# A planner's rule for VectorE and GpSimd, widened to VectorE's copies and tensor_scalars from SBUF

## The chip, the cores and the metric

The kernel runs on one core of a Trainium2 chip. The metric is the device time of one execution in microseconds (us); of several runs the median counts.

## What is computed

Two post-norm layers of a diffusion backbone over 512 latent tokens and 256 context tokens, 1024 wide, in 32-bit floats. Cut to what matters here:

```python
for l in range(2):
    hx, hc = modulate(xs, x_sh1, x_sc1), modulate(cs, c_sh1, c_sc1)   # shifts and scales from c, c_ctx @ w_ada
    aq, ak, av, bq, bk, bv, cq, ck, cv = split_proj(hx @ w_in[l])     # the same for hc
    aq, ak, bq, bk = rope_2d(...)                                     # latent tokens only
    ya = window_gqa(aq, ak, av, akc, avc, sink[l])                    # group A, 6 heads of 64
    yb = diff_attention_latent(bq, bk, bv, bkc, bvc, lam, ...)        # group B, 4 heads of 2 x 32
    yc = neighbourhood_attention(cq, ck, cv, ckc, cvc, na_bias[l])    # group C, 6 heads of 64
    xn = post_norm(xs, concat(ya, yb, yc) @ w_o[l], ...)
    xs = post_norm(xn, swiglu(modulate(xn, ...), w_ffn_in[l], w_ffn_out[l]), ...)
    if l == 0: cs = the same for the context tokens
```

## The kernel before

Activations lie transposed in SBUF, features on the partitions. The large tile R holds every operand of the projections as a pair of rounded numbers, a high part and a low part (what the rounding left), so that a product takes three TensorE passes: high x high, high x low, low x high (`gemm_step`, line 618). A weight block of 128x1024 comes by DMA into WRB or V; ScalarE rounds it into R and GpSimd subtracts to get the low part (`halves`, lines 583 to 588). This subtract is called a split below; it is on GpSimd alone.

Per layer the stages are: the projections of a group of heads (`proj`, line 798) and its attention (`attend`, line 1025), A, then B, then C, overlapped with each other; the output projection; LayerNorm; the feed-forward network. In `proj`, each head's result in PSUM, or after the rotation in the tile TRB, becomes a unit of R in three steps: ScalarE copies it with rounding (the high part; lines 858 and 869), that high part is copied once more within R (`va.tensor_copy`, lines 859 and 870: "va" means that VectorE or ScalarE may do it), and the low part is a subtract of two operands (lines 860 and 872: "vp" is VectorE or GpSimd, "ve" is VectorE alone). Units of group B have 32 rows, those of A and C 64; latent streams are 512 words wide and context streams 256. In `attend`, VectorE makes the negated maxima of the scores, TensorE transposes them, and a one-row cast (line 1044, again "va") puts them into R for the next matmuls.

No instruction is issued where it is written. Every call is recorded as an `Op` (`Program.add`, line 228) with the engines that may do it and a planned duration for each. `Program.schedule` (line 276) then plays a list schedule: whenever an engine is free, it takes the first operation of that engine's list that is ready. What it finds is the fixed order of each engine's queue. Where TensorE is planned to wait, `keep_busy` puts matmuls of constant data (`mean_w`, issued at line 1408) in, as fillers. So all instructions of the profile carry line 400 (the call in `issue`), the memsets line 398, the fillers line 1408; groups are told apart by their tiles.

For VectorE and GpSimd the planner holds a flag `two`: set where an operation has the operands `in0` and `in1`, both in SBUF. Such an operation is not started on VectorE while such a one is planned to run on GpSimd, nor the other way round if it could go elsewhere; a split, which can't, is started and planned longer by the overlap.

Of the kernel before, what the change touches and what calls it, by code (L numbers as in the profile page):

```python
# [187 lines left out]
class Program:  # L188
# [39 lines left out]
    def add(self, alt, args, kw):  # L228
        o = Op()
        idx = len(self.ops)  # L230
        o.kw = dict(kw)
        if args:
            o.kw["ap"] = args[0]
            o.kw["constant"] = args[1]
        o.key = idx
        o.succ, o.slots = [], []
        pre = set()
        seen = set()
        for k, v in o.kw.items():
            if not isinstance(v, (View, bass.AP)):  # L240
                continue
            if isinstance(v, View) and id(v.slot) not in seen:
                seen.add(id(v.slot))
                o.slots.append(v.slot)
                v.slot.left += 1
            w = k in ("out", "accum_out", "ap")
            for c in self.cells(v):
                if c in self.writer:
                    pre.add(self.writer[c])
                if w:  # L250
                    pre.update(self.readers.get(c, ()))
        for k, v in o.kw.items():
            if not isinstance(v, (View, bass.AP)):
                continue
            w = k in ("out", "accum_out", "ap")
            for c in self.cells(v):
                if w:
                    self.writer[c] = idx
                    self.readers[c] = []
                else:  # L260
                    self.readers.setdefault(c, []).append(idx)
        if self.after is not None:
            pre.add(self.after)
        pre.discard(idx)
        o.wait = len(pre)
        for p in pre:
            self.ops[p].succ.append(idx)
        o.alt = {e: (call, duration(e, call.__name__, o.kw), RANK[e].get(self.kind, 3)) for e, call in alt}
        o.eng = alt[0][0]
        o.ready = 0.0  # L270
        o.two = all(k in o.kw and self.sbuf(o.kw[k]) for k in ("in0", "in1"))
        o.kind = self.kind
        o.start = None
        self.ops.append(o)

    def schedule(self):
        ops = self.ops
        free = {e: 0.0 for e in ENG}
        avail = {e: [] for e in ENG}

        def offer(i):
            for e, (_, _, r) in ops[i].alt.items():
                insort(avail[e], (r, i))
        for i, o in enumerate(ops):
            if o.wait == 0:
                offer(i)
        dma, table = 0.0, 0
        twice = {"dve": 0.0, "pool": 0.0}
        ev = [0.0]
        left = len(ops)  # L290
        t = 0.0
        while left:
            if not ev:
                raise RuntimeError("the schedule is stuck")
            t = heapq.heappop(ev)
            while ev and ev[0] <= t:
                heapq.heappop(ev)
            for e in ENG:
                if free[e] > t:
                    continue  # L300
                got = None
                if len(avail[e]) > 40:
                    avail[e] = [q for q in avail[e] if ops[q[1]].start is None]
                for j, (_, i) in enumerate(avail[e]):
                    o = ops[i]
                    if o.ready > t or o.start is not None:
                        continue

                    if o.two and (e == "dve" and twice["pool"] > t or e == "pool" and twice["dve"] > t and len(o.alt) > 1):
                        continue  # L310
                    places = []
                    ok = True
                    for s in o.slots:
                        if s.place is None:
                            pl = s.ring.find(s, t)
                            if pl is None:
                                ok = False
                                break
                            places.append((s, pl))
                    if ok:  # L320
                        got = j
                        break
                if got is None:
                    continue
                avail[e].pop(got)
                for s, pl in places:
                    s.ring.take(s, pl, t)
                o.start, o.eng = t, e
                o.call, o.dur = o.alt[e][:2]
                if e == "pe" and t < COLD:  # L330
                    o.dur *= 2

                if o.two and e in ("dve", "pool"):
                    x = "pool" if e == "dve" else "dve"
                    o.dur += max(twice[x] - t, 0.0)
                    twice[e] = t + o.dur
                left -= 1
                if e == "sp":
                    free[e] = t + 0.5
                    dma = max(dma, t + 1.1) + o.dur  # L340
                    o.end = dma + 0.8
                else:
                    if e == "act":
                        f = TABLE.get(o.kw.get("func"), table)
                        if f != table:
                            table = f
                            o.dur += 1.28
                    free[e] = o.end = t + o.dur
                heapq.heappush(ev, free[e])
                for s in o.slots:  # L350
                    s.left -= 1
                    s.t = max(s.t, o.end + 0.2)
                    if s.left == 0:
                        s.ring.release(s, s.t)
                        heapq.heappush(ev, s.t)
                for q in o.succ:
                    n = ops[q]
                    n.wait -= 1
                    n.ready = max(n.ready, o.end + SYNC[e].get(n.eng, 0.0))
                    if n.wait == 0:  # L360
                        offer(q)
                        heapq.heappush(ev, n.ready)
        self.end = max(o.end for o in ops)
# [54 lines left out]
def duration(eng, name, kw):  # L418

    out = kw["out"] if "out" in kw else kw["ap"]  # L420
    n = words(out)
    inp = next((kw[k] for k in ("in0", "in_", "rhs") if k in kw), out)
    a = inp.ap if isinstance(inp, View) else inp
    psum = a.space == bass.MemoryType.PSUM
    ptrs = sum(isinstance(kw.get(k), (View, bass.AP)) for k in ("scalar", "scalar1", "scalar2", "bias", "scale"))
    if eng == "pe":
        w = kw["lhsT"] if "lhsT" in kw else kw["in_"]
        w = w.ap if isinstance(w, View) else w
        rows, cols = w.ap[0][1], words(w)
        if name == "transpose":  # L430
            return 0.112
        if a.dtype == F32R:
            return max(n / 2400.0 * (1 if n >= 128 else 4) + 0.0135, 0.11)
        if a.dtype == BF16:
            return n / 2400.0 + 0.0135
        if cols < 128:
            return n * 4 / 2400.0 * cols / 128 + 0.005
        return 2 * max(n * 2 / 2400.0, 0.107) + 0.01
    if eng == "act":
        return 0.15 + n / 1200.0 + (0 if psum else 0.045) + (0.19 if "accum_out" in kw else 0.0) + 0.04 * ptrs  # L440
    if eng == "dve":
        if name == "reciprocal":
            return 0.07 + n / 160.0
        if name in ("tensor_scalar", "tensor_copy", "memset") and not psum:
            return 0.13 + n / 1920.0 + 0.06 * ptrs
        return 0.145 + words(inp) / 960.0 + 0.04 * ptrs + (0.08 if "accum_out" in kw else 0.0)
    if eng == "pool":
        if name == "tensor_tensor":
            return 0.25 + n / 464.0
        return 0.25 + n / 500.0 + 0.083 * max(0, ptrs - 1)  # L450
    return max(math.prod(q[1] for q in list((out.ap if isinstance(out, View) else out).ap)) * 4 / 360000.0, 0.05)
# [1069 lines left out]
```

## Time and profile before

| | |
|---|---|
| median of 3 runs | 1905.76 us (1905.16 to 1906.55) |
| the profiled execution | 1907.67 us, of which the span of the core is 1905.9 us |
| TensorE matmuls busy | 1856.6 us, 97% of the span |
| VectorE busy | 988.7 us, 52% |
| ScalarE busy | 758.1 us, 40% |
| GpSimd busy | 620.5 us, 33% |
| the chain that ended last | TensorE 88%, VectorE 6%, ScalarE 2% |
| mean granted clock of TensorE | 0.99 of full speed |

The busy times are shares of one execution. The engines are named PE (TensorE's matmuls), PEld (its weight loads), DVE (VectorE), ACT (ScalarE), POOL (GpSimd) and SP (SyncE, which issues the DMAs). A copy whose output is the rounded type is called CAST. The fillers are in TensorE's busy time. The time of one instruction runs from its start on the engine to its end, with whatever it waits for inside.

### The profile page before, as it was taken

To read this page: it belongs to the slowest core of one execution; us is meant where nothing else is said; L and a number is where in the kernel's file an instruction comes from. 1 tells how busy PE (TensorE), PEld (TensorE's weight loads), DVE (VectorE), ACT (ScalarE), POOL (GpSimd) and SP (SyncE) were. 2 spreads that over 40 slices of the span, in tenths; PEclk is the share of its full clock that TensorE was granted. 3 is DMA by queue.
4 is the path that set the end of the run, shared out by engine and by line. 5 is a ranking of instruction groups with operands and counts; after the bars stand their busy time and mean duration, and the time that the engine had idled before them with its cause. 6 is when DMAs were issued, how large, how long until landed. Compare 5 with 4: busy or idle time off the path is not lost.

```text
span 1905.9 us, 26437 instructions
## 1 busy us (share of the span) xinstructions
PE 1856.6 (97%) x10596; PEld 1556.8 (82%) x10596; DVE 988.7 (52%) x1607; ACT 758.1 (40%) x1365; POOL 620.5 (33%) x383
## 2 busy tenths in 40 slices
PE   9999999999999999999999999989999999999996
PEld 8877767788899888888888888766668998888886
DVE  3566645565577887322122695884554742202234
ACT  3456645556353211221122255444455552222232
POOL 0233411112254332233223362530123444444451
PEclk9999999999999999999999999999999999999998
DMA  8321212113224658321221221110114223233321
GB/s 309 97 67 56 86 53 78 41 55 119 89 78 134 188 190 294 113 67 56 67 67 58 65 100 33 42 61 12 34 39 130 82 67 99 92 97 100 100 67 45
DMA packets 52250, 172.72 MB, mean 91 GB/s; under 512 B 5920, under 2 KB 9376, under 8 KB 51744
## 3 DMA queue, kind: packets, MB, share of 16 engines
q1 hardware_dynamic: 52128, 171.04, 27.9%
q8 instruction: 83, 1.36, 0.3%
q14 instruction: 39, 0.32, 0.1%
HBM read 166.82 MB, written 4.19 MB: 90 GB/s over the span
## 4 chain that ended last, share of the span: by engine, by line
PE 88%; DVE 6%; ACT 2%; DMA 1%; issue 1%; POOL 1%; SPq 0%; POOLq 0%; ACTq 0%; DVEq 0%
PE PSB L400 85%; DVE R L400 3%; PE PSB L1408 3%; DVE TRB L400 2%; ACT R L400 1%; DMA WRB<-in_w_ada_dram 1%; ACT TRB L400 1%; DVE OZ L400 1%; DVE PSB L400 0%; DMA OZ<-in_w_ada_dram 0%; POOL OZ L400 0%; DMA WRB<-in_w_in_dram 0%; POOL TRB L400 0%; POOL R L400 0%; SPq L400 0%
## 5 line engine op out<-in xcount | busy, mean ns | idle before, releaser
L400 PE MATMUL PSB<-R 128*128 128x512 f32 (+5 forms) x8266 | 1572.4, 347 | 20.3 <-DVE R L400 10.9
L400 PEld LDWEIGHTS PSB<-R 128*128 128x128 f32 (+2 forms) x8266 | 1311.6, 190 | 226.6 <-issue 25.0
L400 POOL TENSOR_TENSOR R<-V,R 128x1024 fp32r<-128x1024 f32 x99 | 242.5, 2453 | 368.0 <-ACT R L400 362.0
L400 POOL TENSOR_TENSOR R<-WRB,R 128x1024 fp32r<-128x1024 f32 x74 | 180.9, 2446 | 265.3 <-ACT R L400 219.6
L400 ACT ACTIVATE TRB<-PSB 128x512 f32<-128x512 f32 (+2 forms) x337 | 163.1, 523 | 205.6 <-PE PSB L400 198.3
L400 ACT ACTIVATE R<-V 128x1024 fp32r<-128x1024 f32 x100 | 106.0, 1060 | 313.4 <-PE PSB L400 221.6
L400 PE MATMUL PSB<-TRB,V 128*128 128x512 f32 (+2 forms) x560 | 211.1, 509 | 1.0 <-DVE TRB L400 1.0
L400 DVE TENSOR_TENSOR TRB<-TRB,PSB 128x512 f32<-128x512 f32 (+1 forms) x69 | 39.9, 579 | 314.0 <-PE PSB L400 305.7
L400 DVE TENSOR_TENSOR R<-TRB,R 128x256 fp32r<-128x256 f32 (+3 forms) x150 | 168.4, 1130 | 45.8 <-ACT R L400 45.2
L400 PEld LDWEIGHTS PSB<-TRB,V 128*128 128x128 f32 x560 | 102.6, 194 | 69.1 <-issue 45.5
L400 ACT ACTIVATE R<-WRB 128x1024 fp32r<-128x1024 f32 x90 | 95.2, 1058 | 153.3 <-PE PSB L400 129.7
L400 DVE SCALAR_TENSOR_TENSOR OZ<-PSB,gp,OZ 128x512 f32<-128x512 f32 (+1 forms) x104 | 58.5, 584 | 183.1 <-PE PSB L400 183.1
L398 POOL MEMSET R<- 1x512 f32 (+1 forms) x64 | 26.1, 429 | 303.9 <-PE PSB L400 284.7
L400 ACT CAST R<-TRB 128x512 fp32r<-128x512 f32 (+3 forms) x133 | 72.7, 557 | 120.8 <-DVE TRB L400 119.8
L400 DVE CUSTOM_DVE_ANT_0 TRB<-V,RB,sm 128x1024 bf16<-128x1024 f32 x80 | 113.7, 1449 | 11.0 <-DMA V<-in_w_ada_dram 10.7
L400 DVE TENSOR_REDUCE TRB<-PSB 128x1 f32<-128x768 f32 (+1 forms) x92 | 69.3, 785 | 77.9 <-PE PSB L400 76.9
L400 DVE RECIPROCAL TRB<-TRB 128x512 f32<-128x512 f32 (+1 forms) x31 | 84.5, 2728 | 31.7 <-ACT TRB L400 30.4
L400 DVE TENSOR_TENSOR R<-PSB,R 64x256 fp32r<-64x256 f32 (+4 forms) x88 | 39.7, 456 | 86.0 <-ACT R L400 84.8
L400 ACT CAST R<-PSB 64x256 fp32r<-64x256 f32 (+6 forms) x115 | 46.7, 423 | 91.2 <-PE PSB L400 76.2
L400 POOL TENSOR_SCALAR OZ<-OZ,sm 128x256 f32<-128x256 f32 (+1 forms) x44 | 59.1, 1350 | 70.1 <-ACT R L400 58.5
L1408 PE MATMUL PSB<-mean_w 128*128 128x128 f32 x628 | 81.5, 277 | 0.0
L1408 PEld LDWEIGHTS PSB<-mean_w 128*128 128x128 f32 x628 | 76.6, 192 | 3.1 <-issue 1.8
(91 smaller groups left out, 1110.9 us busy)
## 6 DMA issues: line engine op xcount, KB each, us to landing
V<-in_w_fi_dram SPq DMA_DIRECT2D x66, 512.0 KB, 3.5
V<-in_w_ada_dram SPq DMA_DIRECT2D x56, 512.0 KB, 4.7
WRB<-in_w_in_dram SPq DMA_DIRECT2D x40, 512.0 KB, 3.6
V<-in_w_fo_dram SPq DMA_DIRECT2D x34, 512.0 KB, 3.5
WRB<-in_w_ada_dram SPq DMA_DIRECT2D x31, 512.0 KB, 3.5
WRB<-in_w_fi_dram SPq DMA_DIRECT2D x22, 512.0 KB, 3.6
WRB<-in_w_o_dram SPq DMA_DIRECT2D x16, 512.0 KB, 3.6
WRB<-in_w_fo_dram SPq DMA_DIRECT2D x12, 512.0 KB, 3.5
```

The source lines that it names most:

```text
L398: o.call(kw["ap"], kw["constant"])
L400: o.call(**kw)
L1408: prog.issue(lambda b: nc.tensor.matmul(out=PSB[:, 512 * b:512 * b + P], lhsT=mean_w, rhs=mean_w, start=True, stop=True))
```

## The change

The flag becomes a list of engines. An operation with two or more SBUF inputs (`in0`, `in1`, `in_`) counts on both engines, as before. One with a single SBUF input counts on VectorE alone, if it isn't a reciprocal: VectorE's copies and tensor_scalars from SBUF. Such a one is now not started on VectorE while a counted operation is planned to run on GpSimd, and while it runs a counted operation of GpSimd with another choice isn't started; a split that starts beside it is planned longer. GpSimd's own tensor_scalars and memsets are not counted.

```diff
@@ -268,7 +268,11 @@
-        o.two = all(k in o.kw and self.sbuf(o.kw[k]) for k in ("in0", "in1"))
+
+        ins = [o.kw[k] for k in ("in0", "in1", "in_") if k in o.kw]
+        o.two = ()
+        if ins and all(self.sbuf(x) for x in ins):
+            o.two = ("dve", "pool") if len(ins) > 1 else ("dve",) if alt[0][0] != "pe" and alt[0][1].__name__ != "reciprocal" else ()
@@ -306,7 +310,7 @@
-                    if o.two and (e == "dve" and twice["pool"] > t or e == "pool" and twice["dve"] > t and len(o.alt) > 1):
+                    if e in o.two and (e == "dve" and twice["pool"] > t or e == "pool" and twice["dve"] > t and len(o.alt) > 1):
                         continue
@@ -330,7 +334,7 @@
-                if o.two and e in ("dve", "pool"):
+                if e in o.two:
                     x = "pool" if e == "dve" else "dve"
                     o.dur += max(twice[x] - t, 0.0)
                     twice[e] = t + o.dur
```

What the planner makes of it, as the order of the instructions shows: of the copies within R, 21 fewer on VectorE and 21 more on ScalarE (32x512: 26 and 6 before, 9 and 23 now; 64x512: 23 and 17 before, 19 and 21 now; the 256-wide ones change by one each). Of the low-part subtracts from TRB, 23 go from GpSimd to VectorE (32x512: 22 and 10 before, 2 and 30 now; 64x512: 9 and 7 before, 6 and 10 now). 4 one-row casts of maxima go from ScalarE to VectorE. The fillers are 302, before 314. SP issues 364 instructions in both. In the rows below a number at the end is a count; the lines have moved by 4.

First place: VectorE in layer 0, the first A heads (ISA are the two halves of a maximum with a mask; COPY R<-R is the copy of a high part, CAST R<-PSB the one-row cast of line 1044). Before:

```order
L400 ISA PSB,TRB<-PSB,MK,nsink 128x640
L400 ISA TRB 128x1
L400 COPY R<-R 64x512
L400 ISA PSB,TRB<-PSB,MK,nsink 128x512
L400 ISA TRB 128x1
L400 COPY R<-R 64x512
L400 COPY R<-R 64x256
L400 TENSOR_TENSOR R<-PSB,R 64x256 x2
L400 CAST R<-PSB 1x512
```

Now:

```order
L404 ISA PSB,TRB<-PSB,MK,nsink 128x640
L404 ISA TRB 128x1
L404 ISA PSB,TRB<-PSB,MK,nsink 128x512
L404 ISA TRB 128x1
L404 CAST R<-PSB 1x512 x2
L404 TENSOR_TENSOR R<-PSB,R 64x256 x2
```

The three copies are gone to ScalarE; the casts stand right behind the maxima, and there are two of them.

Second place: VectorE in layer 1, the first B heads (R<-TRB,R and R<-PSB,R are low-part subtracts). Before:

```order
L400 STREAM_SHUFFLE TRB<-PSB 128x512
L400 TENSOR_TENSOR TRB<-PSB,RB 128x512
L400 COPY R<-R 32x512 x3
L400 COPY R<-R 32x256
L400 TENSOR_TENSOR R<-PSB,R 32x256
L400 COPY R<-R 32x256
L400 TENSOR_TENSOR R<-PSB,R 32x256
L400 COPY R<-R 32x512
```

Now:

```order
L404 COPY R<-R 32x512
L404 TENSOR_TENSOR R<-TRB,R 32x512 x2
L404 SCALAR_TENSOR_TENSOR TRB<-MK,TRB 128x128 x2
L404 SCALAR_TENSOR_TENSOR TRB<-MK,TRB 128x2x128 x4
L404 COPY R<-R 32x512
L404 TENSOR_TENSOR R<-TRB,R 32x512
L404 COPY R<-R 32x512
L404 TENSOR_TENSOR R<-TRB,R 32x512 x3
```

The copies stand singly, and the subtracts that GpSimd did before are between them.

Third place: TensorE in layer 0, the first B pair (PSB<-R 128x512 then 128x256 are a pair of score matmuls for the maxima, cs and sel those of the modulation vector, mean_w the fillers; other PSB<-R 128x512 are the projections). Before:

```order
L400 MATMUL PSB<-R 128x512
L1408 MATMUL PSB<-mean_w 128x128 x2
L400 MATMUL PSB<-sel,TRB 128x2
L400 MATMUL PSB<-R 128x512
L400 MATMUL PSB<-R 128x256
L1408 MATMUL PSB<-mean_w 128x128 x6
```

Now:

```order
L404 MATMUL PSB<-R 128x512 x10
L404 MATMUL PSB<-R 128x256
L404 MATMUL PSB<-R 128x512
L404 MATMUL PSB<-WRB,cs_73 32x128 x3
L404 MATMUL PSB<-R 128x512
L404 MATMUL PSB<-R 128x256
L404 MATMUL PSB<-WRB,cs_73 32x128 x5
L404 MATMUL PSB<-R 128x512 x4
L404 MATMUL PSB<-R 128x256
```

Between the score matmuls stand projections and no fillers: 32 of layer 0's B stage are gone; 20 stand in the A and B stages of layer 1 that weren't there before.

## Rows read from the trace of the kernel before

**Rows 1.** The page: the span, and each engine's busy time and instructions.

```profile
span 1905.9 us, 26437 instructions
PE 1856.6 (97%) x10596; PEld 1556.8 (82%) x10596; DVE 988.7 (52%) x1607; ACT 758.1 (40%) x1365; POOL 620.5 (33%) x383
```

**Rows 2.** Groups by shape: form xcount | busy us, mean ns | idle before <-releasers.

```profile
L400 DVE TENSOR_TENSOR R<-TRB,R 128x512 fp32r<-128x512 f32 x65 | 82.8, 1273 | 25.7 <-ACT R L400 25.6
L1408 PE MATMUL PSB<-mean_w 128*128 128x128 f32 x628 | 81.5, 277 | 0.0
...
L400 POOL TENSOR_TENSOR R<-TRB,R 32x512 fp32r<-32x512 f32 x22 | 29.8, 1353 | 31.6 <-ACT R L400 30.5
...
L400 DVE CAST R<-R 32x512 fp32r<-32x512 f32 x26 | 21.2, 817 | 2.6 <-ACT R L400 2.0
...
L400 DVE CAST R<-R 64x512 fp32r<-64x512 f32 x23 | 13.4, 584 | 3.1 <-ACT R L400 2.9
...
L400 DVE CAST R<-R 32x256 fp32r<-32x256 f32 x8 | 10.7, 1337 | 0.2
...
L400 DVE CAST R<-R 64x256 fp32r<-64x256 f32 x10 | 8.1, 821 | 3.6 <-PE PSB L400 3.5
...
L400 ACT CAST R<-R 32x512 fp32r<-32x512 f32 x6 | 3.7, 619 | 0.1
```

**Rows 3.** VectorE in order of time: start us, us, instruction, [idle before <-releaser].

```profile
95.52 4.04 DVE L400 CAST R<-R 64x512 fp32r<-64x512 f32 x2 [0.60 <-ACT R L400]
...
100.46 0.69 DVE L400 CAST R<-PSB 1x512 fp32r<-1x512 f32 x1
...
1200.36 4.05 DVE L400 CAST R<-R 64x512 fp32r<-64x512 f32 x2 [0.94 <-ACT R L400]
...
1206.44 0.28 DVE L400 CAST R<-R 32x256 fp32r<-32x256 f32 x1
...
1211.55 0.68 DVE L400 TENSOR_TENSOR R<-TRB,R 32x512 fp32r<-32x512 f32 x1
...
1233.54 5.68 DVE L400 CAST R<-R 32x512 fp32r<-32x512 f32 x4
...
1239.66 1.97 DVE L400 CAST R<-R 32x256 fp32r<-32x256 f32 x1
...
1242.08 0.42 DVE L400 CAST R<-R 32x512 fp32r<-32x512 f32 x1
```

**Rows 4.** GpSimd in order of time, the splits beside two of those copies.

```profile
97.05 2.36 POOL L400 TENSOR_TENSOR R<-WRB,R 128x1024 fp32r<-128x1024 f32 x1
...
1239.15 2.34 POOL L400 TENSOR_TENSOR R<-WRB,R 128x1024 fp32r<-128x1024 f32 x1
```

**Rows 5.** TensorE in order of time, five instructions that ended an idle time.

```profile
101.20 0.79 PE L400 MATMUL PSB<-R 65*128 65x512 f32 x1 [3.07 <-DVE R L400]
...
410.43 0.44 PE L400 MATMUL PSB<-ident,TRB 128*128 128x128 f32 x2 [1.86 <-ACT V L400]
...
1190.66 1.03 PE L400 MATMUL PSB<-R 128*128 128x256 f32 x5 [0.73 <-DVE R L400]
...
1206.55 0.76 PE L400 MATMUL PSB<-R 65*128 65x512 f32 x1 [3.29 <-DVE R L400]
...
1243.96 0.48 PE L400 MATMUL PSB<-ident,TRB 128*128 128x128 f32 x1 [4.68 <-DVE TRB L400]
```

**Rows 6.** Stretches: us, busy PE PEld DVE ACT POOL (x instructions), granted clock, DMA share, GB/s.

```profile
101.20:107.10 5.90, 5.90 (x11) 3.46 (x12) 0.29 (x1) 2.53 (x5) 0.00 (x0) 0.50 0.16 63
...
1206.60:1213.00 6.40, 6.40 (x12) 3.66 (x13) 4.19 (x7) 3.88 (x7) 1.43 (x1) 0.50 0.08 31
...
1244.00:1247.10 3.10, 3.10 (x9) 2.41 (x10) 1.79 (x4) 0.85 (x2) 0.00 (x0) 0.50 0.00 0
...
1407.56:1410.97 3.41, 3.41 (x11) 3.02 (x12) 2.38 (x4) 3.38 (x7) 0.00 (x0) 0.50 0.54 159
```

## The prediction

> **What bounds the kernel now.** I read the page's busy times first, then the groups of instructions by shape, then the order in time of VectorE, GpSimd and TensorE around the longest waits of TensorE, then the granted clock in stretches. The page shows TensorE busy for 1856.6 of 1905.9 us [rows 1]. So an edit of VectorE, ScalarE or GpSimd can gain only in three ways: through TensorE's idle time (1905.9 - 1856.6 = 49.3 us), through the filler matmuls that the planner puts where it expects TensorE to wait (line 1408, 628 records for 314 instructions, 81.5 us, so 0.26 us each [rows 2]), and through stretches in which TensorE is granted the lower of its two clocks.
>
> The change is about VectorE's copies from SBUF to SBUF inside R, which the profile calls CAST. The groups by shape show them far slower than they need be. A copy of 512 words a partition that meets nothing takes 0.42 us, one of 256 words 0.28 us [rows 3], but the means are 0.817 (26 of 32x512), 0.584 (23 of 64x512), 1.337 (8 of 32x256) and 0.821 us (10 of 64x256) [rows 2]. The surplus is 26 x 0.397 + 23 x 0.164 + 8 x 1.057 + 10 x 0.541 = 10.3 + 3.8 + 8.5 + 5.4 = 28.0 us of VectorE's time.
>
> Where it goes is seen by laying VectorE's and GpSimd's rows beside each other. Two copies start at 95.52 and are done 4.04 us later, at 99.56; GpSimd's split of a weight block runs from 97.05 to 99.41 [rows 3, 4]. The copy ends 0.15 us after the split: it waited for it. At 1239.66 a copy of 256 words takes 1.97 us and ends at 1241.63; the split beside it ends at 1241.49 [rows 3, 4]. The planner of before counts such a meeting only for operations with two SBUF inputs, and so plans these copies at their undisturbed price.
>
> TensorE pays for three of these meetings, as its own rows show [rows 5]:
> - at 101.20 it has been idle for 3.07 us, waiting for VectorE. The two copies took 4.04 instead of 0.42 + 0.28 us, a surplus of 3.34, and the row of maxima that TensorE needs (a 1x512 cast) stood behind them [rows 3].
> - at 1206.55 it has been idle for 3.29 us. The two copies at 1200.36 took 4.05 instead of 0.70: 3.35 too much [rows 3].
> - at 1243.96 it has been idle for 4.68 us. Four copies at 1233.54 (three of 512 words, one of 256) took 5.68 instead of 1.54, and the one at 1239.66 took 1.97 instead of 0.28: 5.83 too much [rows 3].
>
> Surplus and idle time agree in size at each place. A second price follows each: after the idle time the granted clock reads 0.50, the lower level of 1.2 GHz, for 5.90, 6.40 and 3.10 us, with TensorE busy throughout [rows 6]. At half speed half of that is lost: 2.95 + 3.20 + 1.55 = 7.7 us.
>
> **The change part by part.**
> Copies that leave VectorE. The order lists hold 21 copies fewer on VectorE (17 of 32x512, 4 of 64x512; one 32x256 more and one 64x256 less cancel), and 21 more on ScalarE. ScalarE takes 0.62 us for one [rows 2]: 21 x 0.62 = 13.0 us more there, less 4 one-row casts of maxima from PSUM that go the other way. ScalarE is busy for 758 us of the span [rows 1], so most of this lies in its idle time; what it delays is the exponentials queued behind it. I cost it in the last term below.
>
> Subtracts that leave GpSimd. 20 of 32x512 and 3 of 64x512 go from GpSimd (1.35 us for one) to VectorE (0.68 us undisturbed [rows 2, 3]): VectorE gains 23 x 0.68 = 15.6 us and gives up 21 x 0.42 = 8.8 us. Its net 6.8 us is less than the 28.0 us of surplus that can go. GpSimd gets 31 us of room; it bounds nothing here.
>
> The first stall (L0, first A heads). The new order of VectorE has no copy between the maxima and the casts; the wait of 3.07 us has nothing left to come from. Gain 3.07 + 2.95 = 6.0 us.
> The second (L1, same place): 3.29 + 3.20 = 6.5 us.
> The third (L1, first B heads): the new order has no row of copies there, only single ones between subtracts, and the others are on ScalarE: 4.68 + 1.55 = 6.2 us.
> A fourth, small: TensorE idle for 0.73 us at 1190.66 on VectorE [rows 5]: 0.7 us.
>
> Fillers. TensorE's list has 302 in place of 314: in layer 0, 32 vanish from the first B pair; in layer 1, 20 come (in A and B stages). Net 12 x 0.26 = 3.1 us gained. Between them real matmuls take the place, as the order shows; were those not ready in time, the cover is gone and up to 32 x 0.26 = 8.3 us return.
>
> Queues moved past. SP issues the same 364 instructions; only bias loads and weight loads swap places in a few spots. I cost this at nothing: the loads keep their buffers, and a load takes about as long whichever goes first. If one came late it would cost about what DMA waits of TensorE cost now, well under 1 us. VectorE's tensor_scalars are counted too, but stay on VectorE in unchanged numbers; nothing.
>
> What is late next. The order stays fixed when the chip departs from the plan, so I expect new waits. The trace has two that have nothing to do with these copies being planned: 1.86 us at 410.43 [rows 5], and a stretch of 3.41 us at clock 0.50 after another [rows 6]. One such new stall costs 1.86 + 3.41 / 2 = 3.6 us. None at all is the lower bound of this cost; three, 10.8 us, the upper. I take one, since most of the surplus that made stalls goes.
>
> Sum: -6.0 - 6.5 - 6.2 - 0.7 - 3.1 + 3.6 = **-18.9 us**. The profiled execution took 1907.67 us, 1.8 more than its span; with the sum it would take 1888.8. It stands 1.9 above the median 1905.76, so the median becomes 1886.9. Its own range: with three new stalls 1894, with none 1883; and as 28.0 - 3.34 - 3.35 - 5.83 = 15.5 us of the surplus lie apart from the three places and may cost something too (an estimate: less than half of it, 6), down to 1877.
>
> On the copies' new place the Trainium skill, page "Perfetto Trace Analysis", section Optimizing Scalar/DVE Operations, says that an operation which VectorE can do in a fast mode is quicker there than on ScalarE, and that moving it may pay only when VectorE is saturated. Undisturbed the rows agree (0.42 against 0.62): by that the 21 moves would cost 21 x 0.20 = 4.2 us. With the wait for GpSimd the row says 0.82 against 0.62, and the trace decides for the move.
>
> **The rivals.**
> *ScalarE becomes what TensorE waits for.* Each of the 21 copies stands in front of an exponential or an accumulator copy. If each delays TensorE by its whole 0.62 us, 13.0 us come back: -18.9 + 13.0 = -5.9, 1899.9 us. For it: ScalarE releases matmuls in just these stages. Against: it is idle for most of the span [rows 1].
>
> *The wait moves to the subtracts, and the kernel is slower.* The 23 subtracts moved to VectorE read two SBUF operands and can meet a split. Subtracts of 128x512 into R take 1.273 us in the mean [rows 2] where the same number of words takes 0.68 [rows 3]: 0.59 us of waiting each. Today's 28.0 us of waiting cost TensorE 11.0 + 0.7 + 7.7 = 19.4 us, or 0.69 per us. If all copies stopped waiting and each of the 23 waited w, the bill is 23 x w x 0.69 - 19.4 - 3.1; it turns positive above w = 1.42 us. At a whole split, 2.36 us [rows 4], it is +15.0: 1920.8 us. Against: the mean wait of 0.59 is well below 1.42, and the planner has kept two-input subtracts away from GpSimd's all along. The Trainium skill, page "SBUF — State Buffer", section Who interferes with whom, states just this: a VectorE instruction with two SBUF inputs contends with a GpSimd one that reads SBUF. By that alone the subtract is no safer than the copy.
>
> *The change doesn't keep copies and splits apart.* The plan is only a plan: where VectorE runs late, a copy planned before a split meets it anyway, and 46 copies stay on VectorE. If half of the 19.4 us that it costs TensorE stays and three new stalls come, the sum is -9.7 - 3.1 + 10.8 = -2.0: 1903.8 us. For it: two-input subtracts are planned apart, and still wait 0.59 in the mean.
>
> **How the numbers follow.** Forecast 0.70 at 1886.9 (1877 to 1894); ScalarE 0.15 at about 1900; no separation 0.08 at about 1904; subtracts 0.07, above 1910. A measurement of this kernel tells about 0.2%, 3.8 us, from no change. Faster: 0.70 + 0.15 = 0.85; within: 0.08; slower: 0.07. The range leaves out the last two cases and a little of the ends: 1876 to 1901.
>
> **What would show it.** Right: the copies' mean on VectorE near 0.45 us; no wait over 1 us of TensorE near 98, 1203 and 1240 us, and no 0.50 clock after those; filler records near 604; CAST R<-R of ScalarE up by 21. Wrong: new waits of TensorE of 2 us or more on ScalarE or VectorE in the A and B stages, the clock falling as often as now, or 32x512 subtracts on VectorE at 1.4 us or more.

## The result, and the profile after

The changed kernel takes 1885.23 us (median of 4 runs, 1883.95 to 1885.96), the kernel before 1905.46 us (4 runs): a ratio of 0.9893, 95% interval 0.9876 to 0.9910, so 20.2 us less (17 to 24 by the interval). The forecast was 1886.9 us, 18.9 us less. The profiled execution of the changed kernel took 1884.97 us, against 1907.67 of before. Three executions in the experiments below, of the kernel before (3719.9 us) and of the one with tensor_scalars alone (2054.6 and 3184.6 us), fell in a much slower state and count in no comparison.

The page after, answering to [rows 1]:

```profile
span 1883.2 us, 26361 instructions
PE 1842.6 (98%) x10572; PEld 1549.1 (82%) x10572; DVE 970.4 (52%) x1612; ACT 768.0 (41%) x1382; POOL 589.7 (31%) x361
```

The span is 22.7 us shorter. TensorE's idle time is 1883.2 - 1842.6 = 40.6 us where it was 49.3: 8.7 us gained. The other 14.0 us are gained inside its busy time.

The groups by shape after, answering to [rows 2] (columns as there):

```profile
L1412 PE MATMUL PSB<-mean_w 128*128 128x128 f32 x604 | 79.0, 277 | 0.0
...
L404 DVE TENSOR_TENSOR R<-TRB,R 32x512 fp32r<-32x512 f32 x30 | 21.7, 722 | 0.9 <-ACT R L404 0.2
...
L404 ACT CAST R<-R 32x512 fp32r<-32x512 f32 x23 | 14.2, 617 | 0.5
...
L404 DVE CAST R<-R 64x512 fp32r<-64x512 f32 x19 | 8.1, 425 | 0.6 <-ACT R L404 0.4
...
L404 DVE CAST R<-R 64x256 fp32r<-64x256 f32 x9 | 4.4, 497 | 5.6 <-PE PSB L404 5.5
L404 DVE CAST R<-R 32x512 fp32r<-32x512 f32 x9 | 4.1, 451 | 2.0 <-ACT R L404 1.8
...
L404 DVE CAST R<-R 32x256 fp32r<-32x256 f32 x9 | 2.6, 284 | 3.1 <-ACT R L404 3.0
```

Three of the four groups of copies on VectorE take what they take alone (0.425 and 0.451 us against 0.42; 0.284 against 0.28); of the 28.0 us of waiting 19 x 0.005 + 9 x 0.031 + 9 x 0.217 = 2.3 us are left, most of it in one copy of 64x256 that still meets a split (2.02 us, at 1385.50). The subtracts that came to VectorE run at 0.722 us, near their 0.68. Fillers fell from 81.5 to 79.0 us.

The first of the three places: VectorE after, in order of time (start us, us), and then TensorE.

```profile
93.81 0.14 DVE L404 DVE_READ_ACCUMULATOR2_ANT TRB<- 128x1 f32 x1
95.95 1.40 DVE L404 CAST R<-PSB 1x512 fp32r<-1x512 f32 x2 [2.00 <-PE PSB L404]
```

```profile
95.67 2.79 PE L404 MATMUL PSB<-R 128*128 128x512 f32 x11
98.30 0.39 PE L404 MATMUL PSB<-R,BR 65*128 65x512 f32 x1
```

VectorE now waits for TensorE (2.00 us) and not the other way round; TensorE goes on without a gap where it was idle for 3.07 us [rows 5].

The stretches at the lower clock in which TensorE has work, first of before (six and their sum), then after, where there are two (columns as in [rows 6]):

```profile
100.26:107.08 6.82, 5.88 (x11) 3.46 (x12) 1.14 (x3) 2.53 (x5) 0.00 (x0) 0.50 0.26 77
410.87:414.28 3.41, 3.41 (x17) 3.41 (x18) 3.38 (x2) 1.87 (x6) 0.30 (x1) 0.50 0.00 0
1206.17:1213.00 6.83, 6.45 (x12) 3.74 (x13) 4.59 (x8) 4.04 (x7) 1.43 (x1) 0.50 0.13 53
1243.72:1247.13 3.41, 3.17 (x9) 2.48 (x10) 2.10 (x6) 0.88 (x2) 0.00 (x0) 0.50 0.00 0
1407.56:1410.97 3.41, 3.41 (x11) 3.02 (x12) 2.38 (x4) 3.38 (x7) 0.00 (x0) 0.50 0.54 159
1438.28:1441.69 3.41, 3.41 (x9) 1.86 (x8) 2.83 (x5) 2.16 (x5) 0.00 (x0) 0.50 0.86 293
sum 27.29, PE 25.73 PEld 17.98 DVE 16.43 ACT 14.85 POOL 1.73; mean PE 4.29 PEld 3.00 DVE 2.74 ACT 2.48 POOL 0.29
```

```profile
189.28:192.69 3.41, 3.41 (x8) 2.19 (x8) 1.24 (x6) 1.21 (x3) 0.00 (x0) 0.50 0.00 0
400.91:404.31 3.40, 3.40 (x15) 3.13 (x14) 3.37 (x6) 1.27 (x3) 1.87 (x3) 0.50 0.00 0
```

27.3 us at 0.50 have become 6.8. TensorE is busy for 25.7 us of the former and for all of the latter; half of the difference, 9.5 us, is time gained (an estimate: at half the clock half of the busy time is lost, and the idle time in the stretches is counted with the idle time). Idle time 8.7, clock 9.5 and fillers 2.5 make 20.7 of the 22.7 us; 2.0 us are unaccounted for.

One stall is new. TensorE after, around 188 us, and ScalarE beside it:

```profile
185.97 0.38 PE L404 MATMUL PSB<-R 128*128 128x256 f32 x1 [0.64 <-DVE TRB L404]
188.33 0.94 PE L404 MATMUL PSB<-R 128*128 128x256 f32 x3 [1.98 <-ACT TRB L404]
...
196.54 1.75 PE L404 MATMUL PSB<-R 128*128 128x512 f32 x6 [1.14 <-ACT mod L404]
```

```profile
183.24 1.27 ACT L404 CAST R<-TRB 32x512 fp32r<-32x512 f32 x2
184.53 1.26 ACT L404 CAST R<-R 32x512 fp32r<-32x512 f32 x2
185.81 0.62 ACT L404 CAST R<-TRB 32x512 fp32r<-32x512 f32 x1
186.45 0.36 ACT L404 CAST R<-PSB 32x256 fp32r<-32x256 f32 x1
186.72 1.04 ACT L404 CAST R<-R 32x512 fp32r<-32x512 f32 x2
187.78 1.04 ACT L404 ACTIVATE TRB<-PSB 128x384 f32<-128x384 f32 x3
```

The exponentials that TensorE waits for (ACTIVATE) stand behind eight copies for the B heads, four of which (R<-R, 32x512) are of the kind that the change moved to ScalarE.

### The profile page after: what moved, and what is told of

The parts are those of the page before. It is cut to its first block, busy times and chain, and to the rows that moved or that the text cites. A ratio compares the mean times of both kernels' runs of the same rounds, so it can differ in the third digit from the quotient of the medians.

```text
span 1883.2 us, 26361 instructions
## 1 busy us (share of the span) xinstructions
PE 1842.6 (98%) x10572; PEld 1549.1 (82%) x10572; DVE 970.4 (52%) x1612; ACT 768.0 (41%) x1382; POOL 589.7 (31%) x361
## 3 DMA queue, kind: packets, MB, share of 16 engines
q8 instruction: 83, 1.36, 0.3%
## 4 chain that ended last, share of the span: by engine, by line
PE 91%; ACT 3%; DMA 2%; DVE 2%; POOL 1%; issue 1%; SPq 0%; POOLq 0%; ACTq 0%
PE PSB L404 88%; PE PSB L1412 2%; ACT R L404 2%; DMA WRB<-in_w_ada_dram 1%; DMA OZ<-in_w_ada_dram 1%; ACT TRB L404 1%; DVE TRB L404 1%; POOL OZ L404 1%; DVE R L404 1%; POOL R L404 1%; DVE OZ L404 0%; DMA WRB<-in_w_in_dram 0%; ACT V L404 0%; POOL TRB L404 0%; SPq L404 0%
## 5 line engine op out<-in xcount | busy, mean ns | idle before, releaser
L404 PE MATMUL PSB<-R 128*128 128x512 f32 (+4 forms) x8266 | 1566.7, 346 | 16.8 <-ACT TRB L404 4.7
L404 DVE TENSOR_TENSOR R<-TRB,R 128x256 fp32r<-128x256 f32 (+3 forms) x173 | 186.0, 1082 | 45.7 <-ACT R L404 44.6
L404 ACT COPY TRB<-PSB 64x512 f32<-64x512 f32 (+4 forms) x122 | 48.1, 401 | 78.2 <-PE PSB L404 75.0
```

Of the source, the lines that this page charges most:

```text
L404: o.call(**kw)
```

## The experiments

The ratios are to the kernel before, timed on the same chip (medians 1905.4 to 1905.7 us).

**Take away the wait and nothing else.** The order of before, with only the copies within R issued as another operation that gives the same result: a maximum over one element.

```diff
             if "ap" in kw:
                 o.call(kw["ap"], kw["constant"])
+            elif o.eng == "dve" and o.call.__name__ == "tensor_copy" and self.sbuf(kw["in_"]):
+                a = kw["in_"]
+                a = bass.AP(tensor=a.tensor, offset=a.offset, ap=[list(q) for q in a.ap] + [[1, 1]])
+                o.call.__self__.tensor_reduce(out=kw["out"], in_=a, axis=AX.X, op=ALU.max)
```

> The order of before, instruction for instruction (314 fillers, 67 copies on VectorE); only the copies are issued as a tensor_reduce over one element, which does the same work on one input at one word a cycle. Theory (the copy's wait for GpSimd's split is what costs): no copy takes more than about 0.75 us, none ends with a split of GpSimd; TensorE's idle times of 3.07, 3.29 and 4.68 us shrink to under 1.5 us each and the 0.50 clock behind them goes; 11 + 0.7 + 7.7 = 19.4 us less, given back 67 x 0.27 = 18 us of VectorE that lies mostly under cover, 3 to 5 us of it at the three places: about 1890 us, 1886 to 1895. Rival (the gain is the new order and its fillers): the order is that of before, so nothing is gained and 18 us of VectorE are lost: 1905 to 1920 us.

1885.72 us, ratio 0.9890 (0.9873 to 0.9906). The groups by shape of this kernel:

```profile
L402 DVE TENSOR_REDUCE R<-R 32x512 fp32r<-32x512 f32 x26 | 17.6, 676 | 1.6 <-ACT R L404 0.9
L402 DVE TENSOR_REDUCE R<-R 64x512 fp32r<-64x512 f32 x23 | 15.6, 676 | 2.8 <-ACT R L404 2.5
...
L402 DVE TENSOR_REDUCE R<-R 32x256 fp32r<-32x256 f32 x8 | 3.3, 406 | 0.2
```

And its first place, VectorE, GpSimd (here a subtract of the heads) and TensorE in order of time:

```profile
98.50 1.00 DVE L402 TENSOR_REDUCE R<-R 64x512 fp32r<-64x512 f32 x2 [0.33 <-ACT R L404]
...
98.54 1.29 POOL L404 TENSOR_TENSOR R<-TRB,R 64x512 fp32r<-64x512 f32 x1 [0.49 <-ACT R L404]
...
98.59 3.52 PE L404 MATMUL PSB<-R 128*128 128x512 f32 x15
101.95 0.40 PE L404 MATMUL PSB<-R,BR 65*128 65x512 f32 x1
```

A copy beside a split, the one that took 1.86 us in the kernel before (at 1188.75 there), VectorE and GpSimd:

```profile
1183.39 0.68 DVE L402 TENSOR_REDUCE R<-R 64x512 fp32r<-64x512 f32 x1
...
1182.58 2.40 POOL L404 TENSOR_TENSOR R<-WRB,R 128x1024 fp32r<-128x1024 f32 x1 [1.79 <-ACT R L404]
```

Each copy of 512 words takes the same 0.68 us (0.41 for 256 words), with or without GpSimd beside it: 31 of the 49 run beside a two-input operation of GpSimd, two of these beside a split, and none takes longer. Alone that is 0.26 slower than before, and yet the kernel is as fast as the changed one. The pair that took 4.04 us takes 1.00, and TensorE has no gap. The order and the fillers are those of before, so neither is needed for the gain: the wait is what cost.

**Only the knowledge, without the choice.** Copies on VectorE alone (`va` becomes `ve` in lines 859 and 870), once with the old rule and once with the new.

```diff
-                    va.tensor_copy(out=at(r1 if typ == "q" else r2), in_=at(r0))
+                    ve.tensor_copy(out=at(r1 if typ == "q" else r2), in_=at(r0))
-                va.tensor_copy(out=low if typ == "q" else h2, in_=hi)
+                ve.tensor_copy(out=low if typ == "q" else h2, in_=hi)
```

> Before's rule, and the copies within R are VectorE's alone (124 of them). The plan has only 262 fillers. Theory: 124 copies meet splits unplanned; at today's surplus of 0.42 us a copy that is 52 us, at 0.69 us of TensorE per us 36 us against 19.4, so +16.5, less 52 x 0.26 = 13.5 for the fillers: about 1908 us, 1900 to 1920. Rival (fewer fillers, a better order, is the gain): 1905.5 - 13.5 = 1892 us or less.

> The new rule, but the copies within R are VectorE's alone (124): only the planner's knowledge is left, no copy can go to ScalarE. 306 fillers. Theory (keeping copies and splits apart is enough): copies at a mean under 0.5 us, the three stalls gone: -19.4 - 2.1 + 3.6 = -18, about 1888 us, 1882 to 1896. Rival (the gain is ScalarE taking the copies off VectorE): VectorE has 57 x 0.42 = 24 us more to do, TensorE waits for it: 1900 us or more.

With the old rule 1923.06 us, ratio 1.0083 (1.0060 to 1.0106), slower than before in spite of 262 fillers, and above the range I gave; with the new one 1891.97 us, 0.9925 (0.9909 to 0.9942). A copy group of each, old rule first:

```profile
L400 DVE CAST R<-R 32x512 fp32r<-32x512 f32 x32 | 32.1, 1003 | 4.7 <-ACT R L400 4.0
```

```profile
L404 DVE CAST R<-R 32x512 fp32r<-32x512 f32 x32 | 15.0, 469 | 1.2 <-ACT R L404 0.5
```

The same 124 copies on the same engine: 31 us lie between a planner that knows of the wait and one that doesn't. Knowledge alone brings two thirds of the change's gain (13.5 of 20.2 us). The rival shows at one place of the run with the new rule, where TensorE has a longer wait than any of before:

```profile
1211.35 2.04 PE L404 MATMUL PSB<-R 128*128 128x512 f32 x4 [5.68 <-DVE TRB L404]
```

In the 14 us ahead of it VectorE has ten copies in its queue, and subtracts, ahead of the mask that TensorE waits for. Whether the copies alone make that wait isn't shown.

**Only the choice, without the knowledge.** Copies on ScalarE alone (`ac` in the same two lines), old rule.

> Before's rule, and the copies within R are ScalarE's alone (124): no copy can meet a split, whatever the planner knows. 271 fillers. Theory: the waits go with the copies, -19.4 - 43 x 0.26 = -30.6, and ScalarE's 67 x 0.62 = 41.5 us more bring waits of TensorE on ScalarE of the kind seen in the changed kernel (1.98 us idle and 1.7 us of clock), three to five of them, +11 to +18: 1886 to 1893 us. Rival (ScalarE becomes what TensorE waits for): 41.5 us mostly on the path, 1905 us or more.

1876.38 us, ratio 0.9847 (0.9832 to 0.9862): 9 us faster than the changed kernel, and better than I expected. ScalarE is busy for 33.6 us more than before (791.7 against 758.1), not for 41.5, and that costs far less than the rival or I had thought; with TensorE at work the lower clock was granted in two stretches of 3.4 us, as in the changed kernel. Most of the lead over the changed kernel is not a shorter wait: the fillers take 71.6 us there, 7.4 less than in the changed kernel.

**The two halves of the change.** In the new condition, `!= "reciprocal"` is replaced by `not in ("reciprocal", "tensor_copy")` for the first, and by `== "tensor_copy"` for the second.

> Of the change only the half about tensor_scalars: they count on VectorE, copies don't. Copies: 67 on VectorE and 57 on ScalarE, as before; 317 fillers. Theory (the copies are all of it): copies still wait, the three stalls stay in some form: 1905.5 + 3 x 0.26 = 1906 us, 1902 to 1911. Rival (the tensor_scalars of LayerNorm and of the gates carry a part): under 1900 us.

> Of the change only the half about copies: they count on VectorE, tensor_scalars don't. 46 copies on VectorE, 78 on ScalarE, as with the whole change; 299 fillers. Theory: as fast as the whole change, 1885.2 - 3 x 0.26 = 1884.5 us, 1881 to 1888. Rival (the tensor_scalars carry a part): 1890 us or more.

Tensor_scalars alone: 1905.8 us, 1.000 (0.999 to 1.001). Its TensorE, in order of time, has all three stalls:

```profile
101.05 0.79 PE L404 MATMUL PSB<-R 65*128 65x512 f32 x1 [3.08 <-DVE R L404]
...
1205.63 0.47 PE L404 MATMUL PSB<-R 65*128 65x512 f32 x1 [3.29 <-DVE R L404]
...
1243.50 0.35 PE L404 MATMUL PSB<-ident,TRB 128*128 128x128 f32 x1 [4.70 <-DVE TRB L404]
```

Copies alone: 1885.32 us, 0.9892 (0.9877 to 0.9907), the same as the whole. The copies are all of it.

**Is anything of the wait left?** The order of the changed kernel, with the copies issued as in the first experiment.

> The order of the changed kernel, its 46 copies on VectorE issued as a tensor_reduce over one element, which needs no second port. Theory (the change has already kept copies and splits apart): nothing is left to gain; 46 copies are 0.12 to 0.26 us slower, about 10 us of VectorE mostly under cover: 1885 us, 1883 to 1890. Rival (the changed kernel still loses to such meetings): under 1881 us.

1889.72 us, 0.9917 (0.9900 to 0.9934): some 4 us slower than the changed kernel. The waits that are left cost less than slower copies would, and the fast copy is worth having once it doesn't wait.

**Only the subtracts.** The old rule; in lines 860 and 872 `vp` becomes `ve`.

> Before's rule, and the low-part subtracts of the heads (31 on GpSimd before) are VectorE's alone, nothing else: 54 copies on VectorE, 70 on ScalarE, 319 fillers. Theory: most copies waited for GpSimd's subtracts only up to 1.35 us, the long waits were for splits, which stay: part of the 28.0 us of surplus goes, 40 to 70%, so -8 to -14 us, +1.3 for the fillers: 1893 to 1900 us. Rival (moving the subtracts is the whole of it): 1887 us or less; other rival (subtracts that wait in the copies' place): 1906 us or more.

1911.94 us, ratio 1.0033 (1.0021 to 1.0046): my number and the first rival are wrong, the other rival's time is right, but not by its cause. The subtracts don't wait (32 of 32x512 at 0.681 us), and the copies wait less: 10.1 us in all, where it was 28.0. The second and third stall are gone, of the first 1.49 us are left, and TensorE's idle time falls from 49.3 to 46.7 us. What makes the run slower is new waits elsewhere, the clock and more fillers (84.4 us against 81.5). One of the new waits, at 164 us, VectorE first, then TensorE and the clock:

```profile
161.61 2.11 DVE L400 TENSOR_TENSOR R<-TRB,R 32x512 fp32r<-32x512 f32 x3
163.75 0.29 DVE L400 SCALAR_TENSOR_TENSOR TRB<-MK,TRB 128x128 f32<-128x128 f32 x1
```

```profile
164.10 1.22 PE L400 MATMUL PSB<-TRB,V 128*128 128x256 f32 x2 [2.38 <-DVE TRB L400]
```

```profile
159.00:172.70 13.70, 11.32 (x68) 9.04 (x69) 12.54 (x22) 11.01 (x23) 1.62 (x2) 0.50 0.24 77
```

Three subtracts at full speed stand ahead of the mask that TensorE waits for; the lower clock was there from 158.95 us on, before this wait. The longest new wait, 3.37 us at 1271.22, is on ScalarE. All stretches at the lower clock with TensorE at work:

```profile
sum 37.55, PE 35.15 PEld 24.97 DVE 23.24 ACT 19.73 POOL 4.10; mean PE 5.02 PEld 3.57 DVE 3.32 ACT 2.82 POOL 0.59
```

TensorE is busy at 0.50 for 35.15 us, against 25.73 before, which costs 4.7 us. So under the old rule, moving subtracts takes much of the copies' waiting away and is no gain. What the 23 subtracts that the change moved cost or bring under the new rule no run shows: none puts them back on GpSimd.

**Versions that beat both.** The new stall of the changed kernel lies behind copies on ScalarE (eight of them, not seven as the first expectation below says). In the first run below those operations rank behind the exponentials there (the diff without its last added line); in the second on VectorE too; the third has the first rank with the old rule.

```diff
+        if len(alt) > 1 and "act" in o.alt:
+            o.alt["act"] = o.alt["act"][:2] + (5,)
+            o.alt["dve"] = o.alt["dve"][:2] + (5,)
         o.eng = alt[0][0]
```

> The whole change, and on ScalarE the copies and one-row casts that VectorE could do too rank behind the exponentials. 67 copies on VectorE, 57 on ScalarE, 256 fillers (302 with the change). Theory (the change's own new stall, 1.98 us of idle time at 188 us with 0.64 and 1.14 us around it and 1.7 us of clock, comes from seven copies queued ahead of an exponential on ScalarE): that stall goes, -5.5, and 46 x 0.26 = 12 us of fillers: about 1868 us, 1862 to 1876. Rival (copies that come late hold subtracts and score matmuls, so the stall only moves): 1880 us or more.

> The whole change, and the copies and one-row casts that VectorE or ScalarE may do rank behind other work on both engines. 45 copies on VectorE, 79 on ScalarE, 253 fillers. Theory: as the rank on ScalarE alone (1873.2), 3 fillers fewer, and the wait of 3.66 us that TensorE had there on a late copy of VectorE may grow or go: 1868 to 1880 us. Rival (copies late on both engines hold score matmuls): 1880 us or more.

> The rank of the run before last (copies and one-row casts behind the exponentials on ScalarE), but with before's rule. 99 copies on VectorE, 25 on ScalarE, 238 fillers, the fewest of all. Theory (a plan that doesn't know of the wait is worth nothing where copies meet splits): 99 copies at a surplus of 0.3 to 0.5 us each, 30 to 50 us, cost 21 to 35 us of TensorE against 19.4 now; less 76 x 0.26 = 19.8 for the fillers: 1888 to 1905 us, 15 us or more above the same rank with the new rule (1873.2). Rival (the rank made that run fast, not the rule): 1875 us or less.

1873.15 us (0.9829, 0.9814 to 0.9843) with the rank on ScalarE, **1867.09 us (0.9799, 0.9784 to 0.9815)** with the rank on both, 18 us below the changed kernel and a little below the range I gave; and 1897.03 us (0.9958, 0.9944 to 0.9973) with the old rule, although that plan has the fewest fillers of all. There the copies of 32x512 take

```profile
L402 DVE CAST R<-R 32x512 fp32r<-32x512 f32 x27 | 29.5, 1092 | 3.3 <-ACT R L402 2.6
```

so 24 us of difference between equal ranks are the rule's. With the rank on ScalarE alone the stall moved: TensorE waits 3.66 us at 1174.81, behind subtracts of VectorE, two of which take 3.46 us where they need 1.36; a split runs beside them, as the subtract rival had it. VectorE and GpSimd there, in order of time:

```profile
1169.56 3.46 DVE L406 TENSOR_TENSOR R<-TRB,R 32x512 fp32r<-32x512 f32 x2
...
1169.76 2.72 POOL L406 TENSOR_TENSOR R<-WRB,R 128x1024 fp32r<-128x1024 f32 x1 [5.55 <-ACT R L406]
```

So the stall at 188 us went and others came: TensorE's idle time with the rank on ScalarE is 1870.5 - 1830.1 = 40.4 us, where the changed kernel has 40.6, and both have 6.8 us at the lower clock. The 12 us that this run is faster lie in the fillers:

```profile
PE 1830.1 (98%) x10480; PEld 1537.9 (82%) x10480; DVE 970.9 (52%) x1616; ACT 758.6 (41%) x1368; POOL 603.4 (32%) x371
...
L1414 PE MATMUL PSB<-mean_w 128*128 128x128 f32 x512 | 66.0, 277 | 0.0
```

They took 79.0 us in the changed kernel. With the rank on both engines the fillers take as little (65.8 us), no wait is as long as 3.66 us (the longest is 2.16), and the idle time falls to 35.3 us.

## Why the prediction was right

*The price.* The copy's surplus was put down to a wait for GpSimd's split. That it is a wait for GpSimd is right, and shown: issued as a maximum, the same copies in the same order take 0.68 us throughout, and 19.7 us go. That it is the split is less than half of it: counted over the instructions of the trace of before, some 10.6 of the 28.0 us lie beside splits and 15.0 beside GpSimd's low-part subtracts of the heads. At the third place the four copies at 1233.54 stand beside three of these (GpSimd, before):

```profile
1234.85 4.22 POOL L400 TENSOR_TENSOR R<-TRB,R 32x512 fp32r<-32x512 f32 x3
```

The sum isn't touched by this, as it goes by the copies' surplus.

*The three stalls, 18.7 us.* All three are gone; none of the changed kernel's waits of TensorE is longer than 2 us. *The fourth* (0.7) went too.

*The clock.* 7.7 us were forecast for the three places, and as much came there: half of 5.88 + 6.45 + 3.17 us. Three further stretches of 3.4 us at the lower clock were in the trace of before, which the sum didn't touch, at 1407, 1438 and 411 us; the first two went, which is 3.4 us gained, although the idle time of 1.8 us ahead of the first is still there (at 1388 us, now with the clock at 1.00), the third stayed (401 us), and one new one came at 189, which cost 1.7. That the two went wasn't derived.

*Fillers.* 3.1 forecast, 2.5 measured.

*New waits.* One new stall for 3.6 us was assumed, modelled on others. One came: 1.98 us and 1.7 us of clock, with 0.64 and 1.14 us around it, so 5.5. Its cause is that of the ScalarE rival, at one place, not at 21. So the new waits came out 1.9 us dearer than assumed and the fillers 0.6 us less, and the two stretches of clock that the sum had left out gave 3.4 back. That 18.9 lies so near to the measured 20.2 us is in this part luck. The new stall of 1.98 us also lies only just under the 2 us that the prediction named as a sign of being wrong.

*The rule on moving work off VectorE* (the Trainium skill, "Perfetto Trace Analysis", section Optimizing Scalar/DVE Operations) says that an operation with a fast mode on VectorE is quicker there. Alone the copy is (0.42 against 0.62 us); beside GpSimd the trace decided for the move (0.82 against 0.62). The run with all copies on ScalarE, 9 us faster than the changed kernel, fits that, though most of its lead is fewer fillers.

*The rivals.* ScalarE as a bound: no, but a real cost once. Subtracts that wait: hardly in the changed kernel (a mean of 0.722 us), but in the ranked run once. No separation: no, 2.3 us of waiting are left, most of them one meeting.

## What to carry to other kernels

Where a plan fixes the order of the queues, a duration that depends on a neighbour belongs in the plan: here the same copies cost 31 us more when the planner didn't know of the wait, and a plan with fewer expected gaps was slower for it. Compare the mean of a group with its undisturbed rows; where the mean is far above, lay the other engine's rows beside it, and see what stands behind the slow instruction in its queue. Where queues keep a fixed order, work moved to a free engine is paid for by what stands behind it, as at 188 us. A rank for the moved work behind what the bound engine waits for was worth 12 and 18 us here, most of it through fewer fillers. And split a gain into idle time, fillers and clock before putting it down to the stall that one had in mind.

## What was not expected of the hardware

A copy that takes 0.26 us longer but doesn't wait was as good as a planner that avoids the meeting: 0.68 us always for 512 words, against 0.42 alone and up to 1.86 beside GpSimd. And the granted clock weighed as much as the idle time: 27.3 us at the lower level before and 6.8 after are some 9.5 of the 22.7 us gained in the profiled executions, against 8.7 of idle time, and in the run with the subtracts on VectorE one stretch of 13.7 us at the lower level stood where TensorE had waits of no more than 2.4 us. Why a wait of 1.8 us was followed by the lower clock before, and not after, stays open.
